# A list scheduler in the source orders the last gate unit, the attention and both branches

## The chip, the core and the metric

The kernel runs on one core of a Trainium2 chip. Its metric is the device time of one execution in microseconds (us): the median of the runs shown. The core has five engines that work side by side: TensorE (PE in the profile; PEld is its weight load), VectorE (DVE), ScalarE (ACT), GpSimd (POOL) and SyncE (SP), which here only issues transfers between the chip's memory and SBUF. Each engine takes its own instructions in the order in which the program gives them, and waits at one until the work it depends on has signalled. TensorE writes into PSUM banks, which VectorE and ScalarE empty.

## What is computed

One decoder block in float32, for 1024 positions and 1024 channels:

```python
u = rms_norm(h, mix_pre_g)
z = u @ w_in                               # p (512), q, k, v (512 each), gate_a, gate_b (1024 each)
ya = pool_mixer(p) @ w_branch_a            # causal means over 2, 4, 8, 16 positions
# attention: 4 heads, two maps of head dimension 64 each, causal, ALiBi slope per head
a = softmax(q1 @ k1 + bias) - lam * softmax(q2 @ k2 + bias)
o = rms_norm(a @ v, subln_g) * (1 - lambda_init)
yb = o @ w_branch_b
m = sigmoid(gate_a) * ya + sigmoid(gate_b) * yb
h = h + rms_norm(m @ w_out, mix_post_g)
u = rms_norm(h, ffn_pre_g)                 # then a SwiGLU layer of 2816 channels, with its own norm and residual
```

## The kernel before

Float32 operands are split into a high and a low part of a faster type, and each product is made of three matmuls (`triple`, L231 to L235: high by high, high by low, low by high). The large projections go through `seven_steps` (L258), a seven-product scheme of twelve matmuls each over quadrants A11 to A22 and their sums S1 to S4, with accumulators X, Y and Z in three PSUM pools of two banks each: `mm`, `fil` and `pair` (a pair is two banks wide). SBUF work tiles come from two pools, `a8` with 16 slots of 8 KB per partition, and `b4` with 14 slots of 4 KB (L32, L67 to L83).

In order, the program makes the input norm and projection, the query, key and value units (stored to memory as `qkd` and `vd`), the pooled branch's input (`yd`), the gate units (stored as `sgd`), the attention with both branches, the output projection `wo`, and the feed-forward layer. All but the last part of this is placed on the engines by the framework's own ordering or by loops in the source. The stretch that matters here begins with the last gate unit and ends at the first `wo` matmul:

- `load_head` (L632) loads a head's QA and K, then QB and V. K and the Q tiles arrive as transfers into 64 partitions each, 256 KB; V is 1 MB in 128 partitions.
- `last_unit` (L655) is the generator of the last gate unit. Four of its steps go out ahead; then head 0's QB and V are loaded and the table of distances `negd` is made on GpSimd. Its gates are added by VectorE, copied to `g_st` by ScalarE and stored from ScalarE's queue.
- `scores` (L731) makes a block of 128 query rows for both maps: matmuls into a `pair` bank (L750, L751), VectorE's pass that adds the bias and finds the row minimum `nm` (L754), ScalarE's exponential with its sum (L757), and VectorE's combination of the two maps (L761 to L763).
- `transposes` (L770) turns the combined map on TensorE into an `mm` bank (L778); ScalarE and VectorE split it into AT (L780, L89). `values` (L786) multiplies with V (L792), and ScalarE and VectorE write O (L797, L798) and sum its squares.
- `head_norm` (L805) scales a head's O (L811). `turn_head` (L818) transposes it on TensorE (L826) and splits it into OTh and OTl (L828, L829).
- `branch` (L672) makes 16 blocks of 12 matmuls into a `fil` bank, for branch A from y2 (e = 0) and branch B from OT (e = 1). In branch B VectorE multiplies branch A's sum `ma` with one gate, the block with the other, and adds (L162); the two gates come as one tile `sgs`, loaded by `fetch` one block ahead.

The main loop (L889 on) walks the 32 rows of all heads: scores four rows ahead, transposes one row ahead, values. Between their steps `step` (L875) issues triples of `filling` (L833: the rest of the last unit, the y2 loads, branch A, head 1's loads) as shares of a running cost on TensorE and VectorE. Once half of the last head is turned, 16 triples of branch B (four blocks) are mixed in by `ahead` (L864); the other blocks follow after the attention. Then the output weights are loaded and split into `woh` and `wol` (L922 to L931).

Of the kernel before, what the change touches and what calls it, by code (L numbers as in the profile page):

```python
# [3 lines left out]

# [30 lines left out]
LAG = 4  # L35
GATES_AHEAD = 1
WARM = 40
FILLING, LEAD = 0.69, 6.0


@with_exitstack
def block_kernel(ctx, tc, x, w_in, pool_mix, pool_scale, w_branch_a, lam_q1, lam_k1, lam_q2,
# [253 lines left out]

    def half(t):
        return slice(t * HALF, (t + 1) * HALF)
# [330 lines left out]
    heads, attends = {}, {}  # L629
    hs = [slice(0, HD), slice(HD, P)]  # L630

    def load_head(h):  # L632

        QA, K = (a8([P, 2, S], F32R, n) for n in ("QA", "K"))
        for m in range(2):
            r, r2 = hs[m], hs[1 - m]
            nc.sync.dma_start(f32(K[r, m, :]), qkd[h][1][r, 0, :])
            nc.sync.dma_start(f32(K[r2, m, :]), qkd[h][1][r, 1, :])
            for rr in (r, r2):
                nc.sync.dma_start(f32(QA[rr, m, :]), qkd[h][0][r, 0, :])  # L640
        yield
        QB, V = (a8([P, 2, S], F32R, n) for n in ("QB", "V"))
        for m in range(2):
            for rr in hs:
                nc.sync.dma_start(f32(QB[rr, m, :]), qkd[h][0][hs[m], 1, :])
        nc.sync.dma_start(f32(V), vd[h])
        heads[h] = QA, QB, K, V.rearrange("p i (b d) -> p b i d", b=NB)

    head0 = load_head(0)
    for i, pair_cols in enumerate(gate_pairs[:-1]):  # L650
        if i == 3:
            next(head0)
# [8 lines left out]
    negd = b4([P, S], F32, "negd")  # L661
    nc.gpsimd.iota(negd, pattern=[[1, S]], base=-(S - P), channel_multiplier=-1,
                   allow_small_or_imprecise_dtypes=True)
    nc.gpsimd.affine_select(out=negd, in_=negd, compare_op=ALU.is_ge, fill=NEG, base=S - P,
                            pattern=[[-1, S]], channel_multiplier=1)

    def quad_mov(src):
        def mov(t, k):
            return src[k // 2][0][:, k % 2, half(t)], src[k // 2][1][:, k % 2, half(t)]
        return mov  # L670

    def branch(e, w, mov, take):  # L672


        order = [(d, t) for d in range(KD) for t in range(2)]
        if e == 1:
            order[:8] = [(d, t) for t in (1, 0) for d in range(4)]
        ws, sgs = {}, {}

        def fetch(n):  # L680
            if n < len(order):
                d, t = order[n]
                if d not in ws:
                    both = load_w(w[:, d * P:(d + 2) * P], 4, 2 * P, "wb", e == 0)
                    for i in range(2):
                        ws[d + i] = [a[:, :, i * P:(i + 1) * P] for a in both]
                if e == 1:
                    sgs[d, t] = b4([P, 2, HALF], F32, "sgs")
                    nc.sync.dma_start(sgs[d, t], sgd[d][:, :, half(t)])

        for n in range(GATES_AHEAD):
            fetch(n)
        yield
        for n, (d, t) in enumerate(order):
            fetch(n + GATES_AHEAD)
            bh, bl = ws[d]
            sg = sgs.get((d, t))
            if sg is not None:
                tt(ma[t][d // 4][:, d % 4, :], ma[t][d // 4][:, d % 4, :], sg[:, 0], ALU.mult)
# [133 lines left out]
    def filling():  # L833
# [9 lines left out]
        for _ in load_head(1):  # L843
            pass
# [488 lines left out]
```

## Time and profile before

| | us |
|---|---|
| median of the runs | 1273.1 |
| the three runs | 1273.1, 1273.31, 1270.13 |
| span of the profiled execution | 1265.6 |
| TensorE busy in it | 1246.5 |
| VectorE busy | 838.6 |
| ScalarE busy | 582.7 |
| first matmul of the last gate unit's first product | 324.75 |
| first `wo` matmul | 530.12 |

The profile is that of one execution. Its span begins with the first instruction and ends with the last; the measured time has some more around it. Times in the timeline are counted from the start of the span. A row of the timeline gives an instruction's start and how long it is shown as busy. Matmuls are pipelined, so a matmul is shown longer than the time until the next one may start; the price of a matmul on TensorE is the distance between two starts. In brackets stands how long the engine had been idle, and whose signal ended it. The tables of waits sum such idle times by line: the engine and line that waited, the operation that it waited for, us in total, how many, the longest in us.

### The profile page before, as it was taken

The page shows a single profiled execution, that of the slowest core. Times are in us where ns is not written, and L with a number is a line of the kernel's source. Part 1 is how long each engine was busy: PE and PEld are TensorE (multiplying, and loading weights), DVE is VectorE, ACT ScalarE, POOL GpSimd, SP SyncE. Part 2 cuts the span into 40 slices and gives each one's busy share as a digit, 9 for nine tenths or more (in the row PEclk, how much of TensorE's full clock was granted, in tenths as well). Part 3 has the DMA queues.
Part 4 walks back from the last instruction along what each step waited for, and adds up shares of the span by engine and source line. Part 5 has one row for each costly group of instructions (what it writes and reads, how often), then busy time and mean ns, then how long its engine had stood idle before and what let it go on. Part 6 is the DMA issues. An engine that isn't in the chain of part 4 may idle for free.

```text
span 1265.6 us, 15699 instructions
## 1 busy us (share of the span) xinstructions
PE 1246.5 (98%) x5912; PEld 1039.1 (82%) x5912; DVE 838.6 (66%) x1296; ACT 582.7 (46%) x1042; POOL 142.7 (11%) x128
## 2 busy tenths in 40 slices
PE   8999999999999999999999999999999999999997
PEld 7888888888788887888888888888888888888886
DVE  5985784534578888855697655655656547955666
ACT  7553344434477774444553333333333333554542
POOL 4100000000201100000102111011111011000221
PEclk9999999999999999999999999999999999999999
DMA  7354338323797108533314322323322368733236
GB/s 253 114 189 132 135 128 243 115 85 117 259 250 206 34 18 283 169 115 134 117 45 139 125 100 89 103 100 108 125 99 84 125 215 279 238 95 105 87 96 208
DMA packets 135452, 179.15 MB, mean 142 GB/s; under 512 B 7632, under 2 KB 90320, under 8 KB 132944
## 3 DMA queue, kind: packets, MB, share of 16 engines
q1 hardware_dynamic: 124544, 146.56, 37.0%
q10 hardware_dynamic: 10832, 31.59, 6.5%
q8 instruction: 46, 0.75, 0.3%
q14 instruction: 30, 0.25, 0.1%
HBM read 124.39 MB, written 53.74 MB: 141 GB/s over the span
## 4 chain that ended last, share of the span: by engine, by line
PE 89%; DVE 3%; ACT 2%; DMA 2%; issue 2%; POOL 1%; SPq 0%; POOLq 0%; DVEq 0%; ACTq 0%
PE Y L235 10%; PE Y L234 10%; PE Y L233 10%; PE X L235 5%; PE X L234 5%; PE X L233 5%; PE Z L235 3%; PE Z L234 3%; PE Z L233 3%; PE Yd L234 3%; PE Yd L235 3%; PE Yd L233 3%; PE o L792 2%; PE branch L233 2%; PE branch L235 2%; PE branch L234 2%
## 5 line engine op out<-in xcount | busy, mean ns | idle before, releaser
L162 DVE TENSOR_TENSOR p<-Z,p 128x512 f32<-128x512 f32 x35 | 24.2, 691 | 163.3 <-PE Z L235 160.7
L234 PE MATMUL Y<-A_lo,Wh 128*128 128x512 f32 x296 | 115.5, 390 | 0.3 <-DVE A_lo L89 0.3
L233 PE MATMUL Y<-A_hi,Wh 128*128 128x512 f32 x296 | 115.2, 389 | 0.0
L235 PE MATMUL Y<-A_hi,Wl 128*128 128x512 f32 x296 | 115.2, 389 | 0.0
L233 PE MATMUL Y<-S_hi,Wh 128*128 128x512 f32 x280 | 109.2, 390 | 0.0
L233 PE MATMUL X<-S_hi,Wh 128*128 128x512 f32 x280 | 109.2, 390 | 0.0
L235 PE MATMUL Y<-S_hi,Wl 128*128 128x512 f32 x280 | 109.1, 390 | 0.0
L234 PE MATMUL Y<-S_lo,Wh 128*128 128x512 f32 x280 | 109.1, 390 | 0.0
L235 PE MATMUL X<-S_hi,Wl 128*128 128x512 f32 x280 | 108.9, 389 | 0.0
L234 PE MATMUL X<-S_lo,Wh 128*128 128x512 f32 x280 | 108.9, 389 | 0.0
L202 ACT CAST Wh<-wf_t 128x1024 fp32r<-128x1024 f32 x70 | 72.8, 1053 | 72.1 <-PE X L234 30.6
L202 ACT CAST Wh<-w_raw 128x1024 fp32r<-128x1024 f32 x72 | 60.6, 843 | 66.7 <-PE Z L234 40.0
L89 DVE TENSOR_TENSOR w_op<-wd,w_op 128x512 fp32r<-128x512 f32 x77 | 56.1, 729 | 52.8 <-ACT w_op L166 52.6
L89 DVE TENSOR_TENSOR Wl<-wf_t,Wh 128x1024 fp32r<-128x1024 f32 x70 | 86.6, 1245 | 4.8 <-ACT Wh L202 4.8
L166 ACT CAST w_op<-wd 128x512 fp32r<-128x512 f32 x77 | 47.9, 622 | 78.1 <-PE Yd L235 31.4
L89 DVE TENSOR_TENSOR Wl<-w_raw,Wh 128x1024 fp32r<-128x1024 f32 x72 | 70.4, 977 | 14.5 <-ACT Wh L202 14.5
L233 PE MATMUL Yd<-w_op,s_op 128*128 128x512 f32 x176 | 68.7, 390 | 0.6 <-ACT w_op L166 0.6
L234 PE MATMUL Yd<-w_op,s_op 128*128 128x512 f32 x176 | 68.7, 390 | 0.3 <-DVE w_op L89 0.3
L235 PE MATMUL Yd<-w_op,s_op 128*128 128x512 f32 x176 | 68.3, 389 | 0.0
L162 DVE TENSOR_TENSOR wf_t<-w_raw,wf_t 128x512 f32<-128x512 f32 x70 | 65.7, 938 | 1.1
L234 PEld LDWEIGHTS Y<-A_lo,Wh 128*128 128x128 f32 x296 | 55.6, 188 | 12.1 <-DVE A_lo L89 0.7
L233 PEld LDWEIGHTS Y<-A_hi,Wh 128*128 128x128 f32 x296 | 55.6, 188 | 11.6
(269 smaller groups left out, 3058.7 us busy)
## 6 DMA issues: line engine op xcount, KB each, us to landing
s_raw<-fsd SPq DMA_DIRECT2D x35, 512.0 KB, 3.6
w_raw<-in_w_in_dram SPq DMA_DIRECT2D x32, 512.0 KB, 4.3
w_raw<-in_w_ffn_gate_dram SPq DMA_DIRECT2D x22, 512.0 KB, 3.8
w_raw<-in_w_ffn_up_dram SPq DMA_DIRECT2D x22, 512.0 KB, 3.8
fsd<-fss SPq DMA_DIRECT2D x11, 1024.0 KB, 3.9
wd<-in_w_ffn_down_dram SPq DMA_DIRECT2D x44, 256.0 KB, 5.4
fsd<-F SPq DMA_DIRECT2D x33, 256.0 KB, 2.3
qkd<-qk_st ACTq DMA_DIRECT2D x16, 512.0 KB, 3.8
```

What stands on the lines that cost most here:

```text
L89: nc.vector.tensor_tensor(out=o, in0=a, in1=f32(hi), op=ALU.subtract)
L162: nc.vector.tensor_tensor(out=o, in0=a, in1=b, op=op)
L166: nc.scalar.copy(hi, a)
L202: nc.scalar.copy(hi, a)
L233: nc.tensor.matmul(o, ah, bh, start=start, stop=False, skip_group_check=goes_on)
L234: nc.tensor.matmul(o, ah, bl, start=False, stop=False, skip_group_check=goes_on)
L235: nc.tensor.matmul(o, al, bh, start=False, stop=stop, skip_group_check=goes_on)
L792: nc.tensor.matmul(o, ats[b // 4][:, j, b % 4 * P:(b % 4 + 1) * P], V[:, b, :, :], start=b == 0 and j == 0, stop=b == qb and j == 1)
```

## The change

The closures `load_head`, `branch`, `scores`, `transposes`, `values`, `head_norm`, `turn_head`, `filling`, `step` and the main loop are removed. In their place a function `mixer` builds a graph of tasks, and a class `Plan` orders it.

Each task has an engine, a cost, the slots that it reads and writes, and a rank. The costs are formulas of the operand's width: `mm_cost` for matmuls, `dve` and `act` for VectorE and ScalarE, 0.38 us for issuing a load, and for its transfer its bytes at 0.36 MB per us and 2.2 us more. A transfer into 64 partitions is priced by its bytes like any other. The tables HOP give what a signal between two engines costs. `room` says when a slot of a pool (CAPS) comes free; some kinds of tile hold slots in reserve. `schedule` runs through time: it takes, of all engines, the task that can start first, and among those of an engine that can start then the one of lowest rank. `emit` issues the tasks in order of their planned starts, and inside `manual_schedule` this is the order on all five engines.

All tasks of the last gate unit, the branch blocks included, are in the chain "fill", which keeps them in their order; they have ranks from 1000 up, so that a row's scores, transposes and values, whose rank is the row's number, go first when they can. The matmuls and their number are the same, and a branch block is still four triples of three matmuls. In the planned order branch A's last block stands right after the last values, then come all 16 blocks of branch B, and the transposes of the last head's half that is done last stand within the second of these. The gates of the last unit are added by VectorE directly into `g_st`, which takes away three ScalarE copies, and they are stored from SyncE's queue. Only QA and K of head 0 are loaded ahead of the stretch (`load_head0`, the first part of `load_head`). The split of the output weights is part of the graph.

```diff
+CAPS = {"mm": 2, "fil": 2, "pair": 2, "b4": B4, "a8": A8, "wraw": 2, "whi": 2, "wlo": 2, "ft": 2, "sg": 2,
+        "small": 20}
+RESERVE = {"E": 2, "gate": 2}
+HOP = {("PE", "PE"): 0.0, ("PE", "SP"): 0.3}
+HOP_FROM = {"PE": 0.21, "ACT": 0.04, "DVE": 0.04, "POOL": 0.09, "SP": 0.0}
+HOP_TO = {"PE": 0.06, "POOL": 0.05, "SP": 0.1}
+OVERLAP = {"DVE": 0.07, "ACT": 0.08}
+PE_RESTART = 0.11
+DMA_LATENCY, DMA_RATE = 2.2, 0.36
...
+    def room(self, t):
+        need = {}
+        for s in t.needs:
+            if s.live:
+                continue
+            if s.kind != "own" and s.pool in self.queues and self.queues[s.pool][0] is not s:
+                return INF
+            if s.pool:
+                n, extra = need.get(s.pool, (0, 0))
+                need[s.pool] = n + 1, max(extra, self.own.get(s.pool, 0) if s.kind == "late" else RESERVE.get(s.kind, 0))
+        at = 0.0
+        for p, (n, extra) in need.items():
+            over = len(self.pools[p]) + n + extra - CAPS[p]
+            if over > 0:
+                times = sorted(INF if s.free_at is None else s.free_at for s in self.pools[p])
+                at = max(at, times[over - 1] if over <= len(times) else INF)
+        return at
...
+    def schedule(self, patience=None):
+        patience = patience or {}
+        free = {e: 0.0 for e in ("PE", "ACT", "DVE", "POOL", "SP")}
+        waiting = {t: len(t.before) for t in self.tasks}
+        open_ = {e: [] for e in free}
+        dma_free, order = 0.0, []
+        for t in self.tasks:
+            if not waiting[t]:
+                open_[t.engine].append((0.0, t))
+        for _ in range(len(self.tasks)):
+            best = None
+            for e, ts in open_.items():
+                f, first = free[e], INF
+                cand = []
+                for ready, t in ts:
+                    at = max(f, ready, self.room(t))
+                    if at < INF:
+                        cand.append((at, t.rank, t))
+                        first = min(first, at)
+                if not cand:
+                    continue
+                lim = first + patience.get(e, 0.0) + 1e-9
+                at, rank, t = min((c for c in cand if c[0] <= lim), key=lambda c: (c[1], c[0]))
+                if best is None or at < best[0]:
+                    best = at, t
+            if best is None:
+                stuck = [(t.engine, t.rank, [s.pool for s in t.needs if not s.live]) for ts in open_.values() for _, t in ts[:6]]
+                raise RuntimeError(f"stuck {stuck} { {p: len(v) for p, v in self.pools.items()} }")
+            at, t = best
+            e = t.engine
+            for s in t.needs:
+                if s.pool and not s.live:
+                    live = self.pools[s.pool]
+                    if len(live) >= CAPS[s.pool]:
+                        live.remove(min((x for x in live if x.free_at is not None), key=lambda x: x.free_at))
+                    live.append(s)
+                    if s.kind == "own":
+                        self.own[s.pool] -= 1
+                    elif s.pool in self.queues:
+                        self.queues[s.pool].pop(0)
+                s.live = True
+            t.start = at
+            if e == "PE" and at > free[e] + 1e-6 and free[e] > 0:
+                t.start = at = at + PE_RESTART
+            t.end = t.landed = at + t.cost
+            free[e] = t.end - min(OVERLAP.get(e, 0.0), t.cost / 2)
+            if e == "SP":
+                dma_free = max(dma_free, t.end) + t.size / DMA_RATE
+                t.landed = dma_free + DMA_LATENCY
+            for s in t.uses:
+                s.left -= 1
+                if s.pool and not s.left:
+                    s.free_at = max(x.landed + self.hop(x, t) for x, _, _ in s.log)
+            open_[e] = [(r, x) for r, x in open_[e] if x is not t]
+            order.append(t)
+            for x in t.after:
+                waiting[x] -= 1
+                if not waiting[x]:
+                    ready = max(b.landed + self.hop(b, x) for b in x.before)
+                    open_[x.engine].append((ready, x))
+        self.order = sorted(order, key=lambda t: t.start)
+        return max(t.end for t in self.tasks)
...
+    def emit(self):
+        for t in self.order:
+            for s in t.needs:
+                if s.value is None:
+                    s.value = s.make()
+            t.fn()
...
+def mm_cost(n):
+    return 0.109 if n <= P else n / 2400 + 0.0133
...
+def dve(n):
+    return 0.155 + n / 955
+
+
+def act(n):
+    return 0.145 + n / 1180
...
+    def product(o, wn, un, new, rank, done=None):
+        (wh, wl), (ah, al) = (W[wn], k.U[un]) if k else ((0, 0), (0, 0))
+        last = None
+        for q in range(4):
+            def fn(q=q):
+                k.triple(o()[:, 0, :] if un in ("S1", "S4") else o(), wh[:, q, :], wl[:, q, :], ah[:, q, :],
+                         al[:, q, :], new and q == 0, q == 3, not new)
+            last = pl.op("PE", TRIPLE, fn, r=[*pairs[wn], *U[un]], w=[o], rank=rank + q / 10, chain="fill")
+        return last
...
+    def gate(e, t, src, add=None):
+        def fn():
+            o, s = st[e]()[:, half(t)], src()
+            s = s[:, 0, :] if src is X else s
+            if add is None:
+                A.copy(o, s)
+            else:
+                tt(o, s, add(), ALU.add)
+        if add is None:
+            pl.op("ACT", act(HALF), fn, r=[src], w=[(st[e], t)], rank=URGENT)
+        else:
+            pl.op("DVE", dve(HALF), fn, r=[src, add], w=[(st[e], t)], rank=URGENT)
+
+    def store(e):
+        b, d = k.unfinished[e] if k else (0, 0)
+        pl.op("SP", 0.4, lambda: nc.sync.dma_start(k.sgd[d][:, b], st[e]()), r=[st[e]], rank=URGENT, size=0.52)
...
+    product(Y, "B11", "A11", True, LU)
+    copy(p1, Y)
...
+    gate(1, 0, X, u2)
+    store(1)
+    product(Y, "T4", "A22", False, LU + 6)
+    gate(0, 1, Y)
+    store(0)
...
+    def dma(o, i, rank, mb, r=(), w=(), behind=None):
+        pl.op("SP", 0.38, lambda: nc.sync.dma_start(o(), i()), r=r, w=w, rank=rank, size=mb, behind=behind)
+
+    def load_qk(h, rank):
+        K, QA = (a8([P, 2, S], F32R, n, "late" if h > 1 else None) for n in ("K", "QA"))
+        for m in range(2):
+            r, r2 = hs[m], hs[1 - m]
+            dma(lambda m=m, r=r: f32(K()[r, m, :]), lambda r=r: k.qkd[h][1][r, 0, :], rank, 0.262, w=[(K, (m, 0))])
+            dma(lambda m=m, r=r2: f32(K()[r, m, :]), lambda r=r: k.qkd[h][1][r, 1, :], rank, 0.262, w=[(K, (m, 1))])
+            for rr in (r, r2):
+                dma(lambda m=m, rr=rr: f32(QA()[rr, m, :]), lambda r=r: k.qkd[h][0][r, 0, :], rank, 0.262,
+                    w=[(QA, (m, rr.start))])
+        return QA, K
...
+    def load_y2(i):
+        if True:
+            y2.append((a8([P, 2, S], F32R, "y2h"), a8([P, 2, S], F32R, "y2l")))
+            for j in range(2):
+                for s, t in enumerate(y2[i]):
+                    dma(lambda t=t, j=j: f32(t()[:, j, :]), lambda i=i, j=j, s=s: k.yd[2 * i + j][:, s, :],
+                        -5.0 + i, 0.52, w=[(t, (j, 0)), (t, (j, 1))])
...
+    def block(t, hi, lo, i, mov, rank):
+        o = bank("fil", "branch")
+        for q in range(4):
+            mh, ml = mov[q // 2]
+
+            def fn(q=q, mh=mh, ml=ml):
+                c = slice(i * P, (i + 1) * P)
+                k.triple(o(), hi()[:, q, c], lo()[:, q, c], mh()[:, q % 2, half(t)], ml()[:, q % 2, half(t)],
+                         q == 0, q == 3, False)
+            pl.op("PE", TRIPLE, fn, r=[hi, lo, (mh, (q % 2, t)), (ml, (q % 2, t))], w=[o], rank=rank + q * .01, chain="fill")
+        return o
...
+    heads[0] = (qa, kk, *load_bv(0, -5.0, lambda: load_y2(0)))
+    load_y2(1)
+    heads[1] = (*load_qk(1, -2.0), *load_bv(1, -1.0))
+    quads = [a8([P, 4, HALF], F32, "ma", "own") for _ in range(4)]
+    ma.extend([quads[0::2], quads[1::2]])
+    n = 0
+    for d in range(0, KD, 2):
+        hi, lo = branch_weights(0, d, lambda: k.w_branch_a, -3.0 + 4 * n / 3)
+        for i in range(2):
+            for t in range(2):
+                o = block(t, hi, lo, i, y2, 2000.0 + n)
+                m, c = ma[t][(d + i) // 4], (d + i) % 4
+                pl.op("ACT", act(HALF), lambda m=m, c=c, o=o: A.copy(m()[:, c, :], o()), r=[o], w=[(m, c)],
+                      rank=URGENT)
+                n += 1
...
+    order = [(d, t) for t in (1, 0) for d in range(4)] + [(d, t) for d in range(4, KD) for t in range(2)]
+    ws = {}
+    for n, (d, t) in enumerate(order):
+        if d not in ws:
+            both = branch_weights(1, d, lambda: k.w_branch_b, 24.0 + n)
+            ws[d], ws[d + 1] = (both, 0), (both, 1)
+        (hi, lo), i = ws[d]
+        sg = b4([P, 2, HALF], F32, "sgs", "gate")
+        r0 = len(seq) + n
+        dma(lambda sg=sg: sg(), lambda d=d, t=t: k.sgd[d][:, :, half(t)], 27.0 + n, 0.52, w=[sg],
+            behind=row_done[min(27 + n, len(seq) - 1)])
+        m, c = ma[t][d // 4], d % 4
+        pl.op("DVE", dve(HALF), lambda m=m, c=c, sg=sg: tt(m()[:, c, :], m()[:, c, :], sg()[:, 0], ALU.mult),
+              r=[(sg, 0)], w=[(m, c)], rank=r0 + 2)
+        if (1, d) in (k.unfinished if k else [(1, 6), (1, 7)]):
+            pl.op("ACT", act(HALF) + .2, lambda sg=sg: A.activation(sg()[:, 1], sg()[:, 1], AF.Sigmoid),
+                  w=[(sg, 1)], rank=r0)
+        o = block(t, hi, lo, i, OT, 3000.0 + n)
+        pl.op("DVE", dve(HALF), lambda o=o, sg=sg: tt(sg()[:, 1], o(), sg()[:, 1], ALU.mult), r=[o],
+              w=[(sg, 1)], rank=URGENT)
+        pl.op("DVE", dve(HALF), lambda m=m, c=c, sg=sg: tt(m()[:, c, :], m()[:, c, :], sg()[:, 1], ALU.add),
+              r=[(sg, 1)], w=[(m, c)], rank=r0 + 1)
...
-    last_unit = seven_steps(weights(*gate_cols(unfinished)), U, gate_done(unfinished))
-    for _ in range(4):
-        next(last_unit)
-    for _ in head0:
-        pass
...
-    filler = filling()
-    second = branch(1, w_branch_b, quad_mov(OT), take_b)
-    second_half = [_ for _ in range(4 * 4)]
...
-    for _ in filler:
-        pass
-    ahead(len(second_half))
-    for _, f in late:
-        f()
-
-    for _ in second:
-        pass
-
-
...
+    plan = Plan()
+    ma, wo = mixer(plan, SimpleNamespace(
+        nc=nc, a8=a8, b4=b4, mm=mm, fil=fil, pair=pair, small=small, wp=wp, cp=cp, name=name, f32=f32, triple=triple,
+        U=U, W=weights(*gate_cols(unfinished)), head0=head0, temp=temp, sub=sub, sumsq=sumsq, mhalf=mhalf, ident=ident,
+        nlam=nlam, sgc=sgc, qkd=qkd, vd=vd, yd=yd, sgd=sgd, unfinished=unfinished, w_branch_a=w_branch_a,
+        w_branch_b=w_branch_b, w_out=w_out))
+    plan.schedule()
+    with tc.manual_schedule(engines={e.engine for e in (nc.tensor, nc.scalar, nc.vector, nc.gpsimd, nc.sync)}):
+        plan.emit()
```

More of the change, by code (lines that the diff above doesn't have):

```diff
@@ L664, in block_kernel @@
[L664 to L699, printed above, removed]
-            if (e, d) in unfinished:
-                nc.scalar.activation(sg[:, 1], sg[:, 1], AF.Sigmoid)
-            o = fil("branch")
-            for k in range(4):
-                triple(o, bh[:, k, :], bl[:, k, :], *mov(t, k), k == 0, k == 3, False)
-                yield
-            take(d, t, o, sg)
```

507 lines of the change are left out of this document (302 added, 205 removed).

## The prediction

> **What bounds the kernel now.** I read the busy table of the page, its slices, and then, for the stage that the change touches, the table by windows, the waits, and the timeline of TensorE at the stage's two ends.
>
> ```profile
> span 1265.6 us, 15699 instructions
> PE 1246.5 (98%) x5912; PEld 1039.1 (82%) x5912; DVE 838.6 (66%) x1296; ACT 582.7 (46%) x1042; POOL 142.7 (11%) x128
> ```
>
> TensorE is busy 98% of the span (the windows below show its clock granted in full, 1.00), so only its gaps can be won unless matmuls go away, and none do: the order of the changed program against the old one has the same matmuls. Everything outside the stretch from the last gate unit to the first `wo` matmul keeps its order on all engines, so the sum is about that stretch. Its ends, and the price of a 512-wide matmul away from any wait (the starts are the first column, us):
>
> ```profile
> 324.75 0.39 PE L233 MATMUL Y<-A_hi,Wh 128*128 128x512 f32 x1
> ...
> 530.12 0.39 PE L969 MATMUL wo<-woh,mh 128*128 128x512 f32 x1
> 560.51 0.39 PE L970 MATMUL wo<-wol,mh 128*128 128x512 f32 x1
> ...
> 561.19 0.39 PE L970 MATMUL wo<-wol,mh 128*128 128x512 f32 x1
> 346.02 0.36 PE L751 MATMUL s<-K,QB 128*128 128x448 f32 x1
> 346.22 0.36 PE L750 MATMUL s<-K,QA 128*128 128x448 f32 x1
> 386.08 0.33 PE L750 MATMUL s<-K,QA 128*128 128x384 f32 x1
> ...
> 386.43 0.34 PE L750 MATMUL s<-K,QA 128*128 128x384 f32 x1
> 360.86 0.30 PE L750 MATMUL s<-K,QA 128*128 128x320 f32 x1
> 361.00 0.31 PE L751 MATMUL s<-K,QB 128*128 128x320 f32 x1
> 356.02 1.90 PE o L792 x16
> 421.11 0.90 PE aT L778 x8
> ```
>
> The stage takes 530.12 - 324.75 = 205.4 us. The intervals between starts give 0.68/3 = 0.227 us for a matmul 512 wide, 0.20 for 448, 0.175 for 384, 0.146 for 320 (over four of them; one interval is 0.14), 1.90/16 = 0.119 for a value matmul (256 wide), and 0.90/8 = 0.112 for a transpose, of which I take 0.11 since the last one of the eight shows its full length. By the program the stage has 516 matmuls of 512, 32 of 448, 48 of 384, 32 of 320, 16 scores of 256, 288 value matmuls, and 192 transposes or 128-wide scores: 117.1 + 6.4 + 8.4 + 4.7 + 1.9 + 34.3 + 21.1 = 193.9 us. So 205.4 - 193.9 = **11.5 us** of this stage is slack: the most that any order can win. Where it lies, first from the windows (columns: PE, PEld, DVE, ACT and POOL busy, granted clock, DMA share, GB/s), then from the waits:
>
> ```profile
> 326.00:340.00 14.00, 12.15 (x54) 9.49 (x52) 4.42 (x7) 5.97 (x8) 6.62 (x4) 1.00 0.96 315
> 360.00:380.00 20.00, 19.51 (x112) 15.75 (x111) 16.46 (x47) 14.43 (x42) 0.00 (x0) 1.00 1.02 254
> 440.00:460.00 20.00, 20.00 (x120) 17.78 (x120) 18.21 (x40) 15.14 (x38) 0.00 (x0) 1.00 0.09 27
> 480.00:500.00 20.00, 17.85 (x99) 14.41 (x98) 16.56 (x39) 7.46 (x27) 2.01 (x2) 1.00 1.03 359
> 500.00:520.00 20.00, 20.00 (x90) 16.53 (x89) 19.90 (x30) 8.37 (x12) 0.00 (x0) 1.00 0.64 211
> PE s L751 <- DMA QB<-qkd: 1.9, 1, 1.9
> PE oT L826 <- DVE O L811: 1.2, 1, 1.2
> PE o L792 <- DVE O L798: 0.8, 2, 0.6
> PE s L750 <- DVE nm L754: 0.7, 3, 0.3
> PE branch L233 <- DVE sgs L162: 0.4, 1, 0.4
> PEld s L750 <- DVE nm L754: 4.7, 14, 0.7
> ```
>
> TensorE misses 14.00 - 12.15 = 1.85 us at the start and 2.15 us in 480 to 500, and there the first, second, third and fifth wait lie. In the middle it looks full, but a late weight load (PEld) spreads the matmuls while each is still shown busy: the fourteen PEld waits for VectorE's score pass are part of that. Against the prices above, the matmul starts between 340 and 480 come 6.0 us late in sum (an estimate from all starts of that stretch), the start 2.0, the end 2.6 and the rest 0.9 us.
>
> **The change, step by step.** *The wait for QB, 2.0 us.*
>
> ```profile
> 332.23 0.39 PE L235 MATMUL Y<-S_hi,Wl 128*128 128x512 f32 x1
> 334.47 0.47 PE L751 MATMUL s<-K,QB 128*128 128x512 f32 x1 [1.85 <-DMA QB<-qkd]
> 304.12 24.53 SPq L96 DMA_DIRECT2D wb_raw<-in_w_branch_a_dram  x3
> 328.75 2.54 SPq L645 DMA_DIRECT2D QB<-qkd  x4
> 329.42 4.92 DMA QB<-qkd
> ```
>
> 334.47 - 332.23 - 0.227 = 2.0 us. SyncE's queue was held by the third `wb_raw` until 328.65. In the new order no third `wb_raw` stands ahead of QB; its first load waits for the last reader of its buffer, the first product's last A11 matmul, at 327.25 + 0.2 = 327.5. That is 1.25 us earlier, without 0.5 MB of weights ahead in the transfers. With the 4.9 us of the chain's row the first QB part is there at 332.4, the second about 1 us on. The first scores now stand 42 matmuls of 512 into the stage, at 324.75 + 42 x 0.227 = 334.3, so the wait goes, and the margin is 0.9 us; I take 2.0 gained (bounds 0.5 and 2.0). Moved past in SyncE's queue is only that `wb_raw`, which branch A needs much later.
>
> *Head 1's operands.* K, QA and QB of head 1 come behind V and y2. With this order head 1's first scores stand 37.2 us of matmuls into the stage, at 361.9 without stalls; in the trace before they ran at 367. What must land by then, from 327.5 on: 14 of the 64-partition loads (QB 4, K and QA 8, two of QB(1)), 0.262 MB each, and 6.3 MB in 128 partitions (V 1.05, y2 4.2, two `wb_raw`).
>
> ```profile
> 341.00:352.00 11.00, 10.90 (x53) 8.43 (x53) 8.75 (x24) 6.54 (x17) 0.00 (x0) 1.00 1.03 355
> 364.00:372.00 8.00, 7.54 (x48) 6.03 (x47) 6.89 (x19) 5.91 (x19) 0.00 (x0) 1.00 1.02 272
> QB<-qkd SPq DMA_DIRECT2D x16, 256.0 KB, 6.0
> ```
>
> Both windows have the transfers saturated (1.03 and 1.02). The first holds mostly y2, at 355 GB/s; the second mostly 64-partition loads, at 272 GB/s, or 0.96 us each. The plan in the source prices all by bytes at 0.36 MB per us, so 0.73 us a load. By the rows: 14 x 0.96 + 6.3/0.355 = 13.4 + 17.7 = 31.1 us, and about 2 us until the first byte: 360.6, so 1.3 us in time, and I cost it at nothing; the bounds are 0 and 14 x 0.23 = 3.2 us, what the plan undercounts. [...]
>
> *The middle, 6.0 us.* The waits for `nm` come from two pair banks in PSUM: a score group must wait until VectorE has read the group two before. In the new order the least matmul work between a bank's reader being fed and its next use grows from 0.77 to 1.33 us, and for the mm banks, which transposes and values use, from 0.22 to 1.04 us. A score pass takes VectorE this long:
>
> ```profile
> L754 DVE CUSTOM_DVE_ANT_0 E<-s,negd 128x1024 f32<-128x1024 f32 x8 | 9.7, 1218 | 10.7 <-PE s L751 10.7
> L162 DVE TENSOR_TENSOR ma<-ma,sgs 128x512 f32<-128x512 f32 x31 | 20.1, 684 | 1.0 <-DMA sgs<-sgd 0.9
> L89 DVE TENSOR_TENSOR wol<-wo_raw,woh 128x1024 fp32r<-128x1024 f32 x5 | 6.1, 1218 | 0.7 <-ACT woh L929 0.7
> L811 DVE TENSOR_TENSOR O<-O,rstd 128x1024 f32<-128x1024 f32 x3 | 3.6, 1216 | 0.0
> ```
>
> So 1.33 us covers one pass of 1.22 us but no queue in front of it, and VectorE stays 83% loaded by my count of its operations there (18.2 of 20 in the window 440 to 460 before). The bounds are 0 (each wait returns elsewhere) and 4.7 us (all `nm` waits go); I take 2.5, about half, because the operations and their load are the same.
>
> *The end, 2.6 us.* The last head's half that is done first (rows 4 to 7) let TensorE stand for VectorE's scale:
>
> ```profile
> 484.94 0.39 PE L235 MATMUL branch<-OTh,wb_lo 128*128 128x512 f32 x1
> 486.49 0.55 PE L826 MATMUL oT<-ident,O 128*128 128x128 f32 x3 [1.16 <-DVE O L811]
> ```
>
> 486.49 - 484.94 - 0.227 = 1.3 us; the value rows (0.8) and the branch row (0.4 shown, 0.5 by the starts) add 1.3. About 2.9 us of matmuls stood between the values of row 4 and these transposes, so the norm chain takes 2.9 + 1.3 = 4.2 us. The new order has 4.5 us there: it just fits, 0.3 us over. Ahead of the other half's transposes stand 27 matmuls of 512 (branch A's last block, branch B's first, one triple), 6.1 us. Behind the last values all 16 blocks of branch B follow, 43.5 us of matmuls, where four blocks had been mixed into the last head. VectorE's own work beside them: 48 operations of 0.684, two weight splits and about five `wol` of 1.218 = 32.8 + 8.5 = 41.3 us, and some 2 us of small ones: 43.3, level with TensorE. The old trace shows such a stretch, 500 to 520: VectorE 19.90 busy of 20, TensorE unbroken. I take 0.5 us of stall left, 2.1 gained (bounds 1.0 lost, should VectorE's count run past TensorE's by that much, and 2.6 gained).
>
> *At nothing:* three ScalarE copies of 0.604 us go (`g_st<-p`, `g_st<-u`), since ScalarE has room in every window; `sgd` stores move from ScalarE's queue to SyncE's, where head 2's loads and the weights stand behind them, and head 2's first scores stand 31 us of matmuls after head 1's. If that cover is gone, a store's wait for its gate add delays K of head 2 by as much.
>
> Sum: 2.0 + 2.5 + 2.1 = 6.6 us of 11.5, and 4.9 stay (middle 3.5, end 0.5, rest 0.9). The profiled span is 1265.6 and the median of the runs 1273.1, 7.5 us above; the three runs lie 3.2 us apart, so 0.3% (3.8 us) is about what can be told from no change. **1273.1 - 6.6 = 1266.5 us.**
>
> **Rivals.** *Head 1 late.* If the 64-partition loads go at their own price and my 1.3 us of room is not there, TensorE stands 3 us at head 1's scores: 1269.5, no measurable change. For it speaks the flat price in the plan, against it the sum above. [...]
>
> *Nothing won.* The order is fixed for all five engines from modelled durations; each wait could return one place later, since VectorE is the second bound throughout. The time is then 1273; the level VectorE load of the end speaks for it, the waits with no bound behind them (QB, oT) against.
>
> *VectorE held by the gates: slower.* In VectorE's fixed order a multiply by `sgs` stands ahead of the branch's own adds and the splits. Its load took long:
>
> ```profile
> sgs<-sgd SPq DMA_DIRECT2D x16, 512.0 KB, 10.2
> ```
>
> A buffer's round is 10.2 us of load, three operations of 0.684 and the block's 2.72 us of matmuls: 15.0 us. With 16 blocks at 2.72 us, six buffers in the rotation suffice; with four, a block takes 3.75 us, and 12 blocks lose 12 us: 1266.5 + 12 = 1278.5. It decides at five buffers. The old order had sixteen loads issued within 18.5 us, so plenty were free; against it also that the load is short when issued alone, against me that the plan prices it 3.6 us. [...]
>
> **Numbers.** Forecast as summed (gain 4 to 9.3): 0.60. Head 1 late: 0.16, mostly within 0.3%. Nothing won: 0.10. Held by the gates, or a like convoy in VectorE: 0.14, slower. Faster by over 0.3%: 0.60 + 0.03 = 0.63; within: 0.13 + 0.08 = 0.21; slower: 0.14 + 0.02 = 0.16. The range reaches from the gains' upper bounds (2.0 + 4.7 + 2.6 = 9.3, so 1263.8) to the rival with nothing won and the fourth of a percent by which runs differ: 1274.5; held by the gates is left out. The likeliest case alone: 1263.8 to 1269.
>
> **What would show it.** The timeline at about 334 has `s<-K,QB` without a wait for the load; the waits have no `oT <- O` above 0.4 us and less than 3 us of PEld for `nm`; first `wo` matmul 198.8 us after the first of the last gate unit. Wrong, if a score of head 1 at about 362 waits for K, QA or QB; if VectorE's `ma` waits for `sgs` above 2 us in sum; if the stage's time is won and `wo` then waits for `wol`.

## The result, and the profile after

| | before | changed |
|---|---|---|
| median of the runs, us | 1272.51 (4 runs) | 1262.86 (4 runs) |
| lowest to highest, us | 1270.13 to 1273.31 | 1261.31 to 1264.52 |
| span of the profiled execution, us | 1265.6 | 1261.0 |
| stage, first matmul of the last gate unit to first `wo` matmul, us | 205.4 | 200.9 |

The ratio on record is 0.9942, 95% interval 0.9925 to 0.996; it is an estimate over the runs and not the quotient of the two medians, which is 0.9924. Two later measurements, each on a chip of its own, gave 0.9955 (0.9939 to 0.9972, a kernel with the same order in this stage, e3) and 0.9964 (0.9952 to 0.9976, f1). By these ratios the changed kernel is 0.4 to 0.6% faster, some 4.5 to 7.5 us; the two spans differ by 4.6 us, of which 4.5 lie inside the stage.

The head of the page after, and the windows of the stage (columns as in the prediction):

```profile
span 1261.0 us, 15705 instructions
PE 1244.0 (99%) x5912; PEld 1042.4 (83%) x5912; DVE 837.3 (66%) x1296; ACT 581.2 (46%) x1039; POOL 144.0 (11%) x128
326.00:340.00 14.00, 14.00 (x63) 11.60 (x62) 4.18 (x7) 7.16 (x10) 4.80 (x2) 1.00 0.97 316
340.00:360.00 20.00, 20.00 (x120) 17.78 (x119) 18.47 (x52) 14.34 (x39) 0.00 (x0) 1.00 1.04 314
360.00:380.00 20.00, 17.68 (x105) 15.38 (x105) 14.53 (x39) 11.76 (x36) 0.00 (x0) 0.91 1.03 267
380.00:400.00 20.00, 18.68 (x118) 16.66 (x117) 18.97 (x48) 15.30 (x44) 4.72 (x2) 1.00 0.62 162
440.00:460.00 20.00, 20.00 (x135) 18.09 (x134) 19.00 (x47) 16.25 (x44) 1.64 (x1) 1.00 0.00 1
480.00:500.00 20.00, 20.00 (x92) 16.57 (x91) 17.22 (x29) 6.83 (x11) 1.32 (x1) 1.00 0.88 310
```

The start is full (14.00 of 14.00, before 12.15), the end is full (20.00, before 17.85), and two windows in the middle are not: 2.3 us are missing in 360 to 380, at a granted clock of 0.91, and 1.3 us in 380 to 400. The waits of TensorE in the stage are only these two and what hangs on them (weight loads that wait along with the first two are left out):

```profile
PE s L254 <- DMA QB<-qkd: 2.3, 1, 2.3
PE o L254 <- DVE AT L655: 1.3, 1, 1.3
PEld aT L481 <- DVE AT L655: 0.3, 2, 0.2
```

All PEld waits for `nm` (4.7 us before) are gone. Against the prices per shape (taken to another digit they add up to 193.8 us, so the old slack is 11.6 and not 11.5) the stage has 7.2 us of slack where it had 11.6: 4.2 at head 1 (2.5 of wait, 1.7 behind it), 1.5 at AT, and 1.5 in small pieces. So two losses that the plan does not know take back 5.7 of the 10.1 us that its order wins. The timeline at the first:

```profile
361.81 0.39 PE L254 MATMUL s<-K,QB 128*128 128x512 f32 x1
362.04 0.40 PE L254 MATMUL s<-K,QA 128*128 128x512 f32 x1
364.76 0.47 PE L254 MATMUL s<-K,QB 128*128 128x512 f32 x1 [2.33 <-DMA QB<-qkd]
...
366.61 0.63 PE L800 MATMUL branch<-y2l,wb_hi 128*128 128x512 f32 x1
367.03 0.63 PE L801 MATMUL branch<-y2h,wb_lo 128*128 128x512 f32 x1
367.46 0.63 PE L254 MATMUL s<-K,QA 128*128 128x512 f32 x1
```

TensorE stands 364.76 - 362.04 - 0.227 = 2.5 us for QB of head 1. Behind it 512-wide matmuls start every 0.42 to 0.43 us instead of 0.227, until 368.7. At the second place VectorE's scale of O and GpSimd's split of `wb_lo` meet:

```profile
391.38 2.40 POOL L385 TENSOR_TENSOR wb_lo<-wb_raw,wb_hi 128x1024 fp32r<-128x1024 f32 x1
391.53 3.34 DVE L257 TENSOR_TENSOR O<-O,rstd 128x1024 f32<-128x1024 f32 x1
394.79 1.15 DVE L655 TENSOR_TENSOR AT<-aT,AT 128x512 fp32r<-128x512 f32 x2
```

The scale takes 3.34 us where the prediction's row has 1.216; it ends 1.1 us after the split.

### The profile page after: what moved, and what is told of

Same layout as the page of the kernel before. It is cut to its first block, busy times and chain, and to the rows that moved or that the text cites. A ratio compares the mean times of both kernels' runs of the same rounds, so it can differ in the third digit from the quotient of the medians.

```text
span 1261.0 us, 15705 instructions
## 1 busy us (share of the span) xinstructions
PE 1244.0 (99%) x5912; PEld 1042.4 (83%) x5912; DVE 837.3 (66%) x1296; ACT 581.2 (46%) x1039; POOL 144.0 (11%) x128
## 4 chain that ended last, share of the span: by engine, by line
PE 89%; DMA 3%; DVE 3%; issue 2%; ACT 1%; POOL 1%; SPq 0%; POOLq 0%; DVEq 0%; ACTq 0%
PE Y L799 10%; PE Y L800 10%; PE Y L801 10%; PE X L799 5%; PE X L801 5%; PE X L800 5%; PE Yd L800 3%; PE Z L801 3%; PE Z L800 3%; PE Yd L801 3%; PE Z L799 3%; PE Yd L799 3%; PE o L254 2%; PE branch L799 2%; PE branch L800 2%; PE branch L801 2%
## 5 line engine op out<-in xcount | busy, mean ns | idle before, releaser
L801 PEld LDWEIGHTS Y<-A_hi,Wl 128*128 128x128 f32 x296 | 55.6, 188 | 11.6
```

The source lines that it names most:

```text
L801: nc.tensor.matmul(o, al, bh, start=False, stop=stop, skip_group_check=goes_on)
```

## The experiments

The theory after the first look: the order itself wins 10 us; the loads of head 1 come late, because loads into 64 partitions cost more than their bytes; the clock falls behind that wait; and VectorE is held by GpSimd. Rivals: the transfers are late for other reasons, the scale waits for `rstd`, and the middle is won by the list's form and not by its prices. Ratios are to the kernel before on the same chip, medians of different chips are not compared; waits and stage times are of one trace each. The code shown is shortened to the lines that matter. `ms` is VectorE's mean of squares of a head's O, `rstd` the factor that GpSimd makes of it, and a half clock is a granted clock of 0.50.

**e1, the kernel before once more.** No edit.

> The kernel before, once more. Its profiled execution has a span of 1265.6 us while its runs took 1270.1 to 1273.3; the changed kernel's has 1261.0 and its own time 1262.8, only 1.8 us more. Theory A: time is span plus about 1.8 us for both kernels, and the execution in the trace before was one of the shorter ones; then a new trace has a span of 1268 to 1271 us and shows 3 to 5 us more stall somewhere, most likely at the wait for QB near 334 us, with a granted clock below 1.00 behind it as the changed kernel shows behind its wait of 2.3 us. Theory B: the old kernel has about 7 us around its span; then the new span is again near 1265.6 and the time near 1273.

Median 1269.37 of ten runs, and the profiled one took 1267.17 with a span of 1265.4. So the time is span plus 1.8 us for the old kernel too, and the 7.5 us that the prediction put around the span were wrong: the trace on which it was built was of an execution some 5 us shorter than the median of the runs beside it. The new trace has the same stalls (QB 1.9, `oT` 1.1), so it does not show what the longer ones lose. Theory A holds for the 1.8 us around the span; the trace of a longer execution that it expected did not come, here or in f4.

**e2, weights later on SyncE's queue.**

```diff
-        dma(lambda: raw(), ..., rank, 0.52, w=[raw])
+        dma(lambda: raw(), ..., rank, 0.52, w=[raw], behind=qb_last[1] if (e, d) == (0, 4) else None)
```

> The third wb_raw load (512 KB) stands behind head 1's QB in SyncE's queue instead of ahead of its K; the order on the other four engines is the same. Theory: head 1's operands come late because the stream of loads is longer than the plan prices it. Without 512 KB ahead, QB lands about 1.3 us earlier, so the wait of 2.3 us falls to about 1.0, and if the half clock behind it needs a wait of 2 us or so, its 1.7 us go too: 3 us less than the changed kernel, near 1260. Rival 1: the half clock does not hang on this wait's length; then 1.3 us less. Rival 2: the transfers are late for another reason (queue, not bytes); then no change.

The fourth `wb_raw`, which waits for the third's turn, moved as well: 1 MB less ahead of head 1. Ratio 0.9925 (0.9899 to 0.9952), median 1260.54. Its profiled execution still has a QB wait of 1.8 us and the half clock behind it; its span is 1260.8, but the other three spans are 1257.9 to 1259.4. On the same chip e3, which keeps the order of the loads up to head 1, has a median of 1264.66. So the bytes ahead do matter, and the size is near the 3 us expected, though the intervals of the two ratios overlap.

**e3, GpSimd's split behind VectorE's scale.**

```diff
+        if h == 0:
+            splits[4].before[scale] = True
+            scale.after.append(splits[4])
```

> GpSimd's third wb_lo split waits for VectorE's scale of head 0's O; all else keeps its order. In the changed kernel that scale took 3.34 us instead of 1.2 while the split ran from 391.4 to 393.8, and TensorE waited 1.3 us for AT behind it. [...] Rival: the scale waits for something else (its rstd comes from GpSimd just before); then it stays at about 3.3 us and nothing is won.

The edit missed. `before` orders tasks in the plan, but between two engines with no common tile it makes no wait in the program: GpSimd's split still ran from 393.8 to 396.2, right behind `rstd`, and the scale took 3.33 us. The order on all engines is the changed kernel's in this stage, but for one load of weights that goes out later. The run is a repeat of the change, ratio 0.9955 (0.9939 to 0.9972), and it shows that the wait for QB varies: 4.6 us here against 2.3.

**e4, the price of a load into 64 partitions.**

```diff
-... rank, 0.262, w=[(QB, (m, rr.start))])
+... rank, 0.40, w=[(QB, (m, rr.start))])      # the same for K and QA, all heads
```

> The plan is told 1.1 us instead of 0.73 us for a load into 64 partitions; it then orders the scores and the fill anew (some 150 rows of TensorE move), everything else is as in the changed kernel. Theory: the stall at head 1 comes from this price alone; the wait for QB(1) goes with its half clock, 4.2 us less than the changed kernel, near 1259. Rival: what is put ahead of the scores is missing as cover later; one or more waits of VectorE's results of 1 to 3 us come back and the gain is 1 to 3 us.

Ratio 0.9933 (0.9906 to 0.996), median 1261.22. The scores of head 1 moved 4 us down the order, and in this trace the loads came 4 us later too: the QB wait is still 2.5 us. A new wait of 1.4 us appears at 423, for AT, where VectorE's `ms` takes 2.20 us instead of 0.17 beside GpSimd's fourth split (422.48 to 424.85). The rival's new waits came, and in this execution, the slowest of four, the price alone did not cure head 1. By the medians on this chip e4 is 3.4 us below e3 (1264.66, the order of the change), between the rival's 1 to 3 and the theory's 4.2.

**e5, the third split on VectorE,** at the plan's place, no other instruction moved.

```diff
-lambda: G.tensor_tensor(out=lo(), in0=raw(), in1=f32(hi()), op=ALU.subtract)
+lambda: (V if d == 4 else G).tensor_tensor(out=lo(), in0=raw(), in1=f32(hi()), op=ALU.subtract)
```

> The third wb_lo split of branch A is issued on VectorE at the place that the plan gave it, just ahead of the scale of head 0's O; GpSimd no longer runs beside that scale. All other instructions keep their order. Theory: the scale took 3.3 us because GpSimd's split held the way to SBUF; then the scale takes 1.2 and the split 1.2, 2.4 together instead of 3.3, and the wait of TensorE for AT behind them falls from 1.3 to about 0.4 us. Rival: the scale waits for rstd; then the pair takes 4.5 us and the wait grows to 2.5.

The timeline of VectorE there, of e5:

```profile
391.85 1.22 DVE L385 TENSOR_TENSOR wb_lo<-wb_raw,wb_hi 128x1024 fp32r<-128x1024 f32 x1
392.99 1.22 DVE L257 TENSOR_TENSOR O<-O,rstd 128x1024 f32<-128x1024 f32 x1
```

Split and scale take 1.22 each, and the wait for AT falls from 1.3 to 0.3 us. So the split on GpSimd had held the scale, and `rstd` had not. That much is shown; by what the split held it, no run shows. The time itself, ratio 0.994 (0.9921 to 0.996), can't tell 1 us.

**e6, both single edits** (e2 and e5).

> Both single edits: third and fourth wb_raw behind head 1's QB on SyncE, and the third split on VectorE. Theory: the two stalls are separate and add; against the changed kernel 3 to 4 us less from the loads and 0.9 us from the split, a ratio to the kernel before near 0.991. Rival: with the wait for QB gone VectorE runs closer behind TensorE and one of the short waits in the middle comes back; then the split brings nothing.

Ratio 0.9909 (0.9888 to 0.993), median 1258.92; stage 198.5 us. The gains add, as far as the intervals tell. In the trace QB waits 1.7 us, with no fall of the clock behind it, and AT 0.3.

**e7, half prices** for VectorE's and ScalarE's operations in the plan.

```diff
 def dve(n):
-    return 0.155 + n / 955
+    return 0.5 * (0.155 + n / 955)      # act(n), the exponential and the combination likewise
```

> The plan is told half of the durations of VectorE's and ScalarE's operations (their formulas times 0.5); some 210 rows of TensorE move. Theory: the middle has lost its waits because the plan knows how long VectorE and ScalarE take; with half prices it asks for results too early, waits for nm, AT and O come back and the middle loses 3 to 6 us against the changed kernel. Rival: the ranks and the list form alone do it (first what can start, the fill behind); then the time stays within 1 us.

Ratio 1.0209 (1.0191 to 1.0227), median 1296.77; the stage takes 234.8 us, 34 more than in the changed kernel's trace and far more than expected. Waits of TensorE in this stage, of e7:

```profile
PE aT L481 <- DVE AT L655: 7.3, 11, 1.6
PE s L254 <- DVE nm L451: 4.4, 10, 0.7
PE aT L481 <- DVE O L510: 4.3, 5, 1.4
PE o L254 <- DVE AT L655: 3.1, 7, 0.7
```

TensorE waits for the scores' `nm`, for AT, and for O in the `mm` banks, all over the attention. The same list with wrong durations is far worse than the old kernel's shares of a running cost (2.1% slower); the rival (form without prices) fell.

**e8, the fill spent early.**

```diff
-o = block(t, hi, lo, i, y2, 2000.0 + n)
+o = block(t, hi, lo, i, y2, 2000.0 + n if n < 13 else n - 100.0)
```

> The last three blocks of branch A (36 matmuls, 8.2 us) go ahead of the attention's tasks as soon as their turn in the fill comes, so none is left to cover the end of the attention; the rest of the plan follows. Theory: the end's 3.3 us were won by fill kept for the norms of the last head; without it TensorE waits for O and AT between the last rows, 3 to 5 us more than the changed kernel. Rival: the blocks of branch B that now come earlier cover it as well; then less than 1 us.

Ratio 0.9962 (0.9949 to 0.9976), median 1265.8. The end loses 2.0 us: two waits for O (0.9) and one for OTl (0.2), with the matmuls that they spread. QB waited 3.5 us in this trace, and 2.9 more were lost behind it at half clock, so the whole time tells less than the waits. The cover at the end is worth 2 us, less than the theory's 3 to 5; branch B's blocks cover a part, as the rival has it.

**f1, the changed kernel again.** No edit.

> The changed kernel once more, as the measure for the other runs on this chip. Its first trace lost 2.5 us at head 1's QB and another 1.7 us behind it at half the granted clock. Theory: the arrival of head 1's loads differs from execution to execution by one to three us, so the wait lies between 1 and 5 us and the time between 1261 and 1266. Rival: the wait is the same each time, and the spread of the times has another place.

Ratio 0.9964 (0.9952 to 0.9976), spans 1260.7 to 1264.9. QB waits 4.2 us, AT 1.3 as before. The variation sits at head 1's loads: 2.3, 4.6 and 4.2 us in three traces of this order.

**f2, head 1's loads in 128 partitions.**

```diff
-dma(lambda ...: f32(K()[r, m, :]), lambda r=r: k.qkd[h][1][r, 0, :], rank, 0.262, ...)      # 64 rows, twice
+dma(lambda m=m: f32(K()[:, m, :]), lambda m=m: k.qkd[1][1][:, m, :], rank, 0.524, ...)      # 128 rows, once
```

> Head 1's K, QA and QB come as six loads of 512 KB into 128 partitions instead of twelve of 256 KB into 64; bytes and all orders are the same. It leaves out that each tile holds the high and the low part of one map: both halves hold rows of both maps, so head 1's scores are not those of the reference. Theory: the way into 64 partitions is narrower; the six loads take 1.3 us each, 7.7 in all instead of 13.2 at 1.1 us, QB is there about 5 us earlier, and the wait of 2.5 us and the half clock behind it go: 1258 to 1259. Rival: the time goes with the bytes (the plan's price) or with how many engines fetch; then QB lands as before and the wait stays.

Ratio 0.9916 (0.9901 to 0.993), median 1258.43. The window of these loads in the changed kernel, then in f2:

```profile
354.00:362.00 8.00, 8.00 (x52) 7.25 (x51) 7.30 (x23) 6.62 (x20) 0.00 (x0) 1.00 1.05 236
```

```profile
353.00:360.50 7.50, 7.50 (x47) 6.65 (x46) 7.16 (x21) 6.41 (x20) 0.00 (x0) 1.00 1.03 416
```

Both are saturated (1.05, 1.03), and the bytes flow at 236 GB/s into 64 partitions and at 416 into 128. Six loads stand for twelve here, so their number changed too; but both are cut into packets of 4 KB, and in these windows the median packet took 0.29 us in the changed kernel and 0.16 in f2, so it is the packet that is slower and not the start of a load. No wait of a matmul for QB is left, and no fall of the clock; AT's 1.3 us is. Shown: the loads are late by their shape.

**f3, all of it in the plan:** 0.40 as in e4, the weights as in e2, and the third and fourth split planned on VectorE.

```diff
-        if e == 0:
+        if e == 0 and d < 4:
             pl.op("POOL", 2.6, ...)
```

> All that was found, put into the plan: a load into 64 partitions priced 1.1 us, the third and fourth wb_raw behind head 1's QB, and their splits planned on VectorE, so that GpSimd's split never runs beside the attention. Theory: the waits at QB and AT go, of the changed kernel's 7.2 us of slack some 1.5 stay, and the time is 1256 to 1258. Rival: the new plan moves some 140 rows of TensorE, and one new wait of 0.5 to 1.5 us appears that its prices do not know, as in the run with the price alone; then 1258 to 1260, no better than the run with both single edits.

Ratio 0.9904 (0.989 to 0.9919), median 1257.55, four runs within 0.7 us. The windows of f3:

```profile
360.00:380.00 20.00, 20.00 (x127) 17.81 (x126) 18.16 (x51) 16.32 (x48) 0.00 (x0) 1.00 1.04 263
380.00:400.00 20.00, 20.00 (x128) 17.94 (x127) 19.25 (x49) 16.36 (x46) 1.65 (x1) 1.00 1.03 259
```

No matmul waits any more in the stage, which takes 195.2 us: 1.4 above the sum of the prices. This version beats both kernels: on the same chip f1 has 0.9952 to 0.9976.

**f4, a third trace of the kernel before.** No edit.

> The kernel before, for another trace. Two traces of it have a clock of 1.00 throughout and spans of 1265.6 and 1265.4, while its other executions go up to 1273 with a mean granted clock of 0.994 to 0.998. Theory: the longer executions lose their time at half clock behind one of the waits (QB at 332, or the pair at 485 to 488); a trace with a clock below 1.00 shows which. Rival: the trace is again of an execution at full clock, and the place stays open.

Again an execution at full clock, span 1266.6, 1.2 us longer than e1's. That part is found: at 485 the gate's load came later. VectorE in f4:

```profile
486.28 0.69 DVE L162 TENSOR_TENSOR ma<-ma,sgs 128x512 f32<-128x512 f32 x1 [2.02 <-DMA sgs<-sgd]
486.88 0.69 DVE L811 TENSOR_TENSOR O<-O,rstd 128x512 f32<-128x512 f32 x1
```

`oT` waits 2.3 us here, 1.2 in the first trace. The rival came: where the executions with a mean clock of 0.995 lose their time stays open: no trace caught one.

## Why the prediction was right, and where it was not

The direction was right, and the size by the ratio: 6.6 us forecast against the 1273.1 of the runs shown, a ratio of 0.9948; measured 0.9942 to 0.9964 in three measurements. The ratio of 0.9942 makes 1265.7 of 1273.1; the median itself, 1262.86, lies 0.9 us below the stated range. That the sum came so near is in part luck: the order won 10.1 us where 6.6 were forecast, and 5.7 went at two places that the sum had at nothing or not at all. The stage took 200.9 us, not 198.8. By terms, from the first trace of each kernel:

| term | won, forecast | won, measured |
|---|---|---|
| start, wait for QB of head 0 | 2.0 | 2.2 |
| middle, waits between 340 and 480 | 2.5 | 4.6 |
| end | 2.1 | 3.3 |
| head 1's operands | 0 | -4.2 |
| GpSimd beside VectorE | none | -1.5 |

*The span against the median* was misread. The 7.5 us are not "around" the span; 1.8 are (e1). The trace showed a short execution. The difference of two traces (4.6) is thus nearer to what the order wins under like conditions, and a part of the runs' difference is what the old kernel loses at times.

*Start.* The step held: `s<-K,QB` at 334 has no wait in the changed kernel. Its margin is thin as said; e2 has 0.1 us of wait there.

*Middle.* The mechanism held, the size was too small. All `nm` waits went, and 1.4 us of small pieces stayed of 6.0. The argument for half, that VectorE's load is the same, does not carry: what counts is the order against its durations, and e7 shows it, 34 us lost with the same operations and wrong prices. (The 83% of load stands beside a window of 18.2 of 20, which is 91%.)

*End.* 3.3 us went where 2.1 were forecast. The working put all of the wait of `oT` down to the norm chain; a part of it was the gates. From the first trace before:

```profile
484.30 1.01 POOL L126 TENSOR_TENSOR rstd<-ms,mhalf 128x4 f32<-128x4 f32 x1 [17.84 <-DVE ms L125]
485.13 0.69 DVE L162 TENSOR_TENSOR ma<-ma,sgs 128x512 f32<-128x512 f32 x1 [0.91 <-DMA sgs<-sgd]
485.74 0.69 DVE L811 TENSOR_TENSOR O<-O,rstd 128x512 f32<-128x512 f32 x1
```

`rstd` is there at 485.31, and in the other half of this head, where VectorE was free, the scale began 0.04 us behind it (493.35, 493.39). So the chain alone lets the scale begin at 485.35. It began 0.4 us later, behind a multiply that had waited for the gates' load: 0.4 of the 1.3 us belong to the gates, 0.9 to the chain. In f4 the same count gives 1.5 us to the gates. The new order issues the first gates at 463.2 instead of 479.1 and has more matmuls ahead of `oT`; no run separates the two. e8 shows that the matmuls kept for the end are worth 2.0 us of it, at the values and at OTl. The rival "VectorE held by the gates" did not come: in the changed kernel no `ma` waits for `sgs`.

*Head 1.* This step failed. "1.3 us in time, and I cost it at nothing": QB was 2.5 us late, and a score at about 362 that waits for it is what the prediction had named as a sign of being wrong. The sum priced a 64-partition load at 0.96 us from a window at 272 GB/s that held other loads too; alone they run at 236 GB/s, 1.1 us each, 14 x 0.15 = 2.1 us more, and another 1.6 are the first load, which took 4.5 us to land where 2 and its own 0.96 were counted (a load of 0.5 KB, `sgc`, took 2.1 us to land in the first trace). Into 64 partitions the loads run at 236 GB/s where f2's run at 416 into 128, a ratio of 0.57; the prediction's two windows, with other loads mixed in, have 272 and 355, a ratio of 0.77. The rival "head 1 late" came true in its mechanism, at 4.2 us where it had 3, and the gain of the rest outweighed it.

*GpSimd beside VectorE* was in no term and in no rival. The old trace had the row: `ms` at 425.44 took 1.19 us instead of 0.17, to 426.63, and a GpSimd split ran from 424.20 to 426.60. The next score pass began right behind it, and TensorE's wait of 0.26 us for that block's `nm` at 428.43 is shorter than the 1.02 us by which `ms` was longer; so it very likely cost a little there too.

*Cost at nothing* held for the copies and the stores, and VectorE's level load in the end cost nothing: TensorE is full from 480 on.

## What to carry to other kernels

A list scheduler in the source is worth its prices: with measured durations it took 10 us of slack out of a stage of 205 (and gave 5.7 back elsewhere), and with halved ones for two engines the stage was 34 us longer. What the list does not model is where the new order pays, so after the first trace look for resources without a line in the plan: here the shape of a load (236 GB/s into 64 partitions, 416 into 128), a GpSimd split beside an operation of VectorE (the scale took 3.34 us instead of 1.22), and the spread of a load's arrival (waits of 2.3 to 4.6 us for QB in three traces of one order). And hold one profiled span against its own execution's time before building a sum on a median.

## What the runs showed of the hardware

*Behind some waits of 1.4 to 4.6 us the granted clock was 0.50.* The windows around the wait of the changed kernel, and around the wait of the old one (the column after POOL is the granted clock):

```profile
362.00:364.00 2.00, 0.44 (x2) 0.00 (x1) 2.00 (x5) 1.18 (x5) 0.00 (x0) 1.00 1.08 254
364.00:366.00 2.00, 1.24 (x5) 0.95 (x6) 0.10 (x1) 0.00 (x0) 0.00 (x0) 0.81 0.98 317
366.00:368.00 2.00, 2.00 (x7) 1.61 (x6) 1.18 (x2) 1.08 (x3) 0.00 (x0) 0.50 0.99 395
```

```profile
332.00:334.00 2.00, 0.62 (x3) 0.19 (x1) 0.00 (x0) 0.00 (x0) 0.69 (x1) 1.00 0.94 236
334.00:336.00 2.00, 1.53 (x7) 1.31 (x8) 0.47 (x1) 0.00 (x0) 0.00 (x0) 1.00 1.10 252
```

A wait of 2.3 us is followed by 3.4 us at 0.50, which cost 1.7 us; waits of 1.9, 1.9 and 2.0 us for QB in three traces of the old kernel are followed by none, one of 1.8 in e2 is, one of 1.7 in e6 is not, nor that of 2.3 for `oT` in f4. Longer waits (2.5, 2.6, 3.5, 4.2, 4.6) had it every time, at a cost of 1.6 to 3 us. And in e7 the clock fell behind a wait of only 1.4 us, at the beginning of another of 0.7:

```profile
440.37:443.79 3.42, 1.67 (x10) 1.07 (x8) 2.71 (x5) 1.74 (x6) 0.00 (x0) 1.00 0.00 0
443.79:447.20 3.41, 3.07 (x12) 3.07 (x13) 3.27 (x10) 2.77 (x6) 0.00 (x0) 0.50 0.02 5
```

So in these traces the length of one wait does not decide. The half clock lasts from 365.26 to 368.67 in the changed kernel and from 443.79 to 447.20 in e7, 3.41 us each. The changed kernel's trace has a second fall, at 1259.55, behind its last matmul, and the old kernel's first trace has one at 1261.68. Counted from the first rise of the clock in its trace (at 6.86 and 5.58 us, where 128-wide matmuls go from 0.213 to 0.109 us apart), the three falls come after 358.40, 1252.69 and 1256.10 us, which are 105, 367 and 368 times 3.4133 us. In the 3.41 us before its fall TensorE was idle for 2.33 us in the changed kernel, and shown busy for 1.67 of 3.42 us in e7. What decides a fall, no run was made to test.

The mean clock of single executions of the old kernel lies between 0.994 and 1.00, and the longest ones have the lowest (on one chip 1274.55 at 0.994 and 1267.17 at 1.00): 0.6% of 1267 us is 7.6 us, about their difference of 7.4. So the spread between its executions is, by its size, such time at half clock. This is an estimate: the last 1 to 4 us of a span, behind the last matmul, are at 0.50 too in these traces, which alone takes up to 0.2% off the mean.

*Beside a GpSimd split, some VectorE operations took longer.* The measured times are 3.34 against 1.22 us (scale), 2.20 against 0.17 (`ms` in e4), and the first is gone in e5, where the split is VectorE's own. The scale ended 1.09 us behind the split (394.87 and 393.78), `ms` in e4 0.03 us behind it (424.88 and 424.85). Others did not take longer: beside the split from 426.62 to 429.03 in the changed kernel VectorE's operations that read PSUM keep their times (AT 0.42, O 0.35, a score pass 0.82 us; in e5, from 395 on and with no split beside them, 0.42, 0.35 and 0.81). What makes the difference, no run was made to test.
